# Output projection on half-precision pairs with run-time scales, in a one-core adaLN mixer block

## The chip, the cores and the metric

One NeuronCore of a Trainium2 chip runs the whole program. The metric is the device time of one execution in microseconds. A run of the kernel before has the median 1238.68 us over three executions (1238.41 to 1240.36).

## What is computed

One layer of a transformer block over 2048 latent and 256 context tokens, width 1024, in fp32. Shortened to what matters here:

```python
u = h @ w_in                                  # h: normalised, modulated x
attn = attend(q, k_all, v_all)                # 4 heads, 2048 queries, 2304 keys
br   = concat([silu(gate_a) * attn, silu(gate_p) * pool(pool_in) * pool_scale], -1)   # (2048, 1024)
y    = br @ w_out                             # the output projection: 2048x1024 by 1024x1024
out  = x + gate * y
```

The change touches the last two lines alone. The matmul engine is fed with two-part operands: each fp32 number is written as hi + lo, and a product is made of three passes (hi hi, hi lo, lo hi).

## The kernel before

The program has three stages that overlap at their edges. The feature stage makes `u` feature by feature (`feat`, 48 matrix steps of 48 matmuls each, in four token groups `b`). Its generators of side work (`plan`) are called at numbered steps; step 24 begins the second token group, and the feature stage has 96 steps. Its weights come in through tiles of tag M (6 buffers), are split into fp16 halves with a run-time scale (`split16`, L238 and L239), and from the third group on come back from DRAM (`wd`). Attention (`attn`, `pv_all`) follows. The tail is the output projection.

In the tail the branch outputs lie in DRAM (`brd`), features on partitions. `load_pair(t2)` (L1137) brings the 256 tokens of one pair of token tiles into a tile of tag B (8 buffers), with the residual `xr`. Pair 0 is computed plainly (`plain_pair`, 8 products); pairs 1 to 7 go through `out_pair` (L1196), a Strassen-like form with 7 products, whose operands are sums of blocks of the branch outputs (`sums_of`, 4 VectorE adds) and of blocks of `w_out` (`wo_sums`, the sums T1 to T4). One product (`products`, L1155) is 4 contraction tiles by 3 passes, 12 matmuls of 128x128 by 128x512. An operand is made by `operand` (L1161): ScalarE copies the source to hi in fp32r (L1163), VectorE subtracts for lo (L1164). The weights go through `wo_pair` (L1043) in the same way (L1051 on ScalarE, L1053 on VectorE), two calls per block and 8 blocks. A product is read from PSUM by a VectorE add (`add`, L1199; L1185 in the plain pair; one ScalarE copy, L1210), and `close` (L1144) multiplies by the gate and adds `xr` on GpSimd (L1150), then stores.

`scale_of` (L224) already exists for the feature stage: a matmul with a matrix of ones over columns of sums of squares (L227), a VectorE reduction and a scalar step (L229, L230) and a power on GpSimd (L231). `unscale` is a product and a reciprocal on VectorE (L234, L235); `square` is a ScalarE pass with an accumulator (L248).

The order of instructions in each engine's queue is not the program's: a planner walks the program in its order of priority with cost estimates of its own and puts on each engine the first instruction that it holds ready. The queues are then fixed, and each engine runs its own in order. `order` adds edges by hand (operands of the tail after the last block of attention). All DMAs are issued by SP, in order.

Of the kernel before, what the change touches and what calls it, by code (L numbers as in the profile page):

```python
# [8 lines left out]
F32 = mybir.dt.float32  # L9
F32R = mybir.dt.float32r  # L10
F16 = mybir.dt.float16
AF = mybir.ActivationFunctionType
ALU = mybir.AluOpType
AX = mybir.AxisListType

S, L, D = 2048, 256, 1024
KT = D // 128
# [28 lines left out]
X_AT = {0: "c", 11: 2}  # L46
PROD_AT = {"c": (6, 2), 2: (16, 1), 4: (35, 3), 6: (54, 1)}
GATE_AT = (25, 3)
TW_AT = (3, 2)
KV_AT = 79  # L50
Q_AT = 87
# [8 lines left out]
K_PF = (3, 5)  # L60
WO_AT = (1, 4, 7, 10, 13, 15, 17, 18)
BR_AT = 16
CHUNKS = ((0, 512), (512, 512), (1024, 512), (1536, 512), (2048, 256))
G_A, G_PIN, G_P = 448, 960, 1472

# [2 lines left out]
def tile_hybrid_block(ctx: ExitStack, tc: tile.TileContext, x, c, cx, c_ctx, w_mod, b_mod, norm_g,  # L68
                      w_in, q_lora_g, w_uq, kv_lora_g, w_ukv, q_norm_g, k_norm_g, w_pool,
                      pool_scale, w_out, rope_t, edge_t, out):  # L70
    nc = tc.nc
    x, cx, out = x[0], cx[0], out[0]
    w_mod, w_in, w_uq, w_ukv, w_pool, w_out = (w[0] for w in (w_mod, w_in, w_uq, w_ukv, w_pool, w_out))
# [15 lines left out]
    def st(tag, shape, dt=F32):  # L89
        return sb.tile([128] + list(shape), dt, tag=tag, bufs=BUFS[tag], name=nm(tag))  # L90
# [48 lines left out]
    ssw = cst.tile([128, 20], F32, name="ssw")  # L139
    scl = cst.tile([128, 16], F32, name="scl")  # L140
    unscl = cst.tile([128, 14], F32, name="unscl")
    acs, shs = cst.tile([128, KT, 2], F32, name="acs"), cst.tile([128, KT, 2], F32, name="shs")

    queue = []
# [76 lines left out]

    def scale_of(c, cols, bound=1.0):  # L224

        p = pt("X")
        nc.tensor.matmul(p[:, 0:cols.stop - cols.start], lhsT=ones2, rhs=ssw[:, cols], start=True, stop=True)  # L227
        t = small(1, "sca")
        nc.vector.reduce_sum(t, p[:, 0:cols.stop - cols.start], axis=AX.X)  # L229
        nc.vector.tensor_scalar(out=t, in0=t, scalar1=bound * 2.0 ** -30, scalar2=1e-30, op0=ALU.mult, op1=ALU.add)  # L230
        nc.gpsimd.tensor_tensor(out=scl[:, c:c + 1], in0=t, in1=nhalf[:, 0:1], op=ALU.pow)  # L231
# [6 lines left out]
        nc.scalar.activation(out=hi, in_=src, func=AF.Copy, scale=scale)  # L238
        nc.vector.scalar_tensor_tensor(out=lo, in0=src, scalar=scale, in1=hi, op0=ALU.mult, op1=ALU.subtract)  # L239

    def square(src, c, scale=1.0):
        n = 1
        for k in src.shape[1:]:
            n *= k
        o = junk[:, 0:n]
        if len(src.shape) == 3:
            o = o.rearrange("p (a b) -> p a b", a=src.shape[1])
        nc.scalar.activation(out=o, in_=src, func=AF.Square, scale=scale, accum_out=ssw[:, c:c + 1])  # L248
# [448 lines left out]
    def feat(b):  # L697
# [6 lines left out]
        for g in range(H):  # L704
# [54 lines left out]
                n0 = n1  # L759
            yield  # L760

    def gate_row():
        acc = st("M", [D])
        for k in range(KT):
            yield
            wr = st("M", [D])
            nc.sync.dma_start(out=wr, in_=w_mod[k * 128:(k + 1) * 128, 2 * D:3 * D])
            if k == 0:
                nc.vector.tensor_scalar(out=acc, in0=wr, scalar1=sc[:, 0:1], scalar2=None, op0=ALU.mult)
            else:  # L770
# [42 lines left out]
    g = gate_row()  # L813
    for i in range(10):
        plan.setdefault(GATE_AT[0] + GATE_AT[1] * i, []).append(g)


    K, V, qop = {}, [], {}
# [218 lines left out]
    def load_wo(a, b):  # L1037
# [2 lines left out]
                          .rearrange("(k p) n -> p k n", p=128))  # L1040
        wraw[a, b] = raw

    def wo_pair(key, raw, tag):  # L1043
        if tag == "W":
            w = st("W", [2, 4, 512], F32R)
            wo[key] = (w[:, 0], w[:, 1])
        else:
            wo[key] = (st("B", [4, 512], F32R), st("B", [4, 512], F32R))
        hi, lo = wo[key]
        for k in (0, 2):  # L1050
            a = nc.scalar.activation(out=hi[:, k:k + 2], in_=raw[:, k:k + 2], func=AF.Copy)  # L1051
            order(tail[-1], a.ins, "the last block of attention comes first")
            nc.vector.tensor_tensor(out=lo[:, k:k + 2], in0=raw[:, k:k + 2], in1=hi[:, k:k + 2].bitcast(F32),  # L1053
                                    op=ALU.subtract)
            yield

    def out_weights():
        for a, b in ((0, 0), (0, 1), (1, 0), (1, 1)):
            yield from wo_pair(f"B{a}{b}", wraw[a, b], "W")
# [98 lines left out]
                nc.tensor.matmul(b[:, c0:c1], lhsT=c[:, x0, kt, :], rhs=w[x1][:, kt, c0:c1],  # L1158
                                 start=(first and kt == kts[0] and m == 0), stop=(last_ and kt == kts[-1] and m == 2))

    def operand(src):  # L1161
        c = st("M", [2, 4, 128], F32R)
        nc.scalar.activation(out=c[:, 0], in_=src, func=AF.Copy)  # L1163
        op_last.append(nc.vector.tensor_tensor(out=c[:, 1], in0=src, in1=c[:, 0].bitcast(F32), op=ALU.subtract).ins)  # L1164
        return c

    def blocks_of(br):
        return {f"A{m}{k}": br[:, 4 * k:4 * k + 4, m * 128:(m + 1) * 128] for m in range(2) for k in range(2)}

    def plain_pair(t2, br, xr):  # L1170

        v = blocks_of(br)
        c = {key: operand(v[key]) for key in ("A00", "A10", "A01", "A11")}
        bank = {}
        yield
        for a in range(2):
            for n in range(2):
                for m in range(2):
                    if a == 0:
                        bank[m, n] = pt("A")  # L1180
                    products(bank[m, n], c[f"A{m}{a}"], wo[f"B{a}{n}"], a == 0, a == 1)
                    yield
                    if a:
                        o = st("T", [512])
                        nc.vector.tensor_tensor(out=o, in0=bank[m, n], in1=g[n], op=ALU.mult)  # L1185
                        close(t2, xr, m, n, o, ops=(ALU.add,))

    def sums_of(br):
# [7 lines left out]
    def out_pair(t2, v, xr, early={}):  # L1196
        def add(b, a, c0=0, c1=512):
            o = st("T", [512])
            nc.vector.tensor_tensor(out=o[:, c0:c1], in0=b[:, c0:c1], in1=a[:, c0:c1], op=ALU.add)  # L1199
            return o  # L1200

        for i, a, b in (FORM if t2 > 1 else [FORM[j] for j in (0, 4, 5, 1, 2, 3, 6)]):
            c = early.pop(a, None) or operand(v[a])
            pb = pt("A")
            cols = ((0, 256), (256, 512)) if t2 == 7 and i == 4 else ((0, 512),)
            for c0, c1 in cols:
                products(pb, c, wo[b], True, True, c0, c1)
            if i == 1:
                p1 = st("T", [512])
                nc.scalar.copy(out=p1, in_=pb)  # L1210
            elif i == 6:
                u = add(pb, p1)
            elif i == 5:
                z = add(pb, u)
                if t2 == 1:
                    close(t2, xr, 0, 1, add(p3, z))
            elif i == 7:
                close(t2, xr, 1, 1, add(pb, z))
                y = add(pb, u)
            elif i == 2:  # L1220
                close(t2, xr, 0, 0, add(pb, p1))
            elif i == 3:
                p3 = pb
                if t2 > 1:
                    close(t2, xr, 0, 1, add(pb, z))
            else:
                for c0, c1 in cols:
                    close(t2, xr, 1, 0, add(pb, y, c0, c1), c0, c1)
            yield
# [25 lines left out]
            step += 1  # L1255
    for _ in at:
        pass
    ow = out_weights()
    gb = st("M", [D])
    nc.sync.dma_start(out=gb, in_=gated.partition_broadcast(128))  # L1260
    g = [gb[:, 0:512], gb[:, 512:1024]]
    for n, _ in enumerate(pg):
        for _ in range(WO_AT.count(n)):
            next(ow)
        if n == BR_AT:
            first = plain_pair(0, *pairs.pop())
            next(first)
# [6 lines left out]
    for n, _ in enumerate(first):  # L1274
        if n == 0:
            br, xr = load_pair(1)
        if n < 3:
            next(sums, None)
        elif n == 3:
            early["A00"], early["A01"] = (operand(blocks_of(br)[key]) for key in ("A00", "A01"))  # L1280
            v = sums_of(br)
        elif n == 5:
            early["S4"] = operand(v["S4"])
        else:
            next(sums, None)
    for _ in sums:
        pass
    for t2 in range(1, 8):
        nxt = None
        for n, _ in enumerate(out_pair(t2, v, xr, early)):  # L1290
            if n == 1 and t2 < 7:
                br, nxr = load_pair(t2 + 1)
            if n == 3 and t2 < 7:
                nv = sums_of(br)
        if t2 < 7:
            v, xr = nv, nxr
# [48 lines left out]
```

## Time and profile before

| | us |
|---|---|
| median of three executions | 1238.68 |
| the profiled execution | 1236.57 |
| its span | 1234.8 |
| feature stage and what precedes it | 0 to about 540 |
| attention | about 500 to 1069 |
| output projection on the matmul engine | 1069.3 to 1229.6 |
| TensorE matmul busy | 1169.2 (95%) |
| VectorE / ScalarE / GpSimd busy | 894.6 / 765.8 / 597.3 |

The span is what the profile covers; 1.8 us lie around it. PE is TensorE's matmuls and PEld its weight loads, DVE is VectorE, ACT ScalarE, POOL GpSimd. Durations of matmuls in the profile overlap, so the pace of a stream is read from starts.

### The profile page before, as it was taken

The page shows a single profiled execution, that of the slowest core. Times are in us where ns is not written, and L with a number is a line of the kernel's source. Part 1 is how long each engine was busy: PE and PEld are TensorE (multiplying, and loading weights), DVE is VectorE, ACT ScalarE, POOL GpSimd, SP SyncE. Part 2 cuts the span into 40 slices and gives each one's busy share as a digit, 9 for nine tenths or more (in the row PEclk, how much of TensorE's full clock was granted, in tenths as well). Part 3 has the DMA queues.
Part 4 walks back from the last instruction along what each step waited for, and adds up shares of the span by engine and source line. Part 5 has one row for each costly group of instructions (what it writes and reads, how often), then busy time and mean ns, then how long its engine had stood idle before and what let it go on. Part 6 is the DMA issues. An engine that isn't in the chain of part 4 may idle for free.

```text
span 1234.8 us, 22505 instructions
## 1 busy us (share of the span) xinstructions
PE 1169.2 (95%) x7717; PEld 871.5 (71%) x7717; DVE 894.6 (72%) x1704; ACT 765.8 (62%) x1860; POOL 597.3 (48%) x670
## 2 busy tenths in 40 slices
PE   6899899989999999989999999999999998799998
PEld 2699796877788879655666666666666655688886
DVE  4965766666545445578788888878887866999886
ACT  4587767645655554367777777777777776633221
POOL 3735512624335332024655565565556565236666
PEclk9799899999999999999999999999999999999999
DMA  9446676496435657458977788878888788525532
GB/s 302 143 118 158 165 194 188 131 250 209 144 97 129 150 159 178 125 125 191 230 191 194 168 220 207 191 169 223 203 188 197 197 215 203 181 76 197 188 130 101
DMA packets 192585, 216.82 MB, mean 176 GB/s; under 512 B 92707, under 2 KB 145236, under 8 KB 192342
## 3 DMA queue, kind: packets, MB, share of 16 engines
q1 hardware_dynamic: 192470, 215.38, 65.7%
q8 instruction: 61, 1.00, 0.4%
q14 instruction: 54, 0.44, 0.1%
HBM read 100.33 MB, written 41.85 MB: 115 GB/s over the span
## 4 chain that ended last, share of the span: by engine, by line
PE 71%; DMA 7%; ACT 7%; DVE 6%; SPq 4%; issue 2%; POOL 1%; ACTq 0%; DVEq 0%; POOLq 0%
PE pA L884 19%; PE pA L690 15%; PE pA L1158 13%; PE pO L933 5%; PE pA L340 5%; PE pX L933 5%; SPq L923 3%; PE pX L884 2%; PE pA L619 2%; ACT M L966 2%; ACT T L905 1%; DMA M<-in_w_in_dram 1%; DVE T L371 1%; DMA W<-W 1%; DMA W<-in_w_mod_dram 1%
## 5 line engine op out<-in xcount | busy, mean ns | idle before, releaser
L970 POOL TENSOR_TENSOR M<-W,M 128x512 f16<-128x512 f32 x244 | 277.7, 1160 | 255.3 <-ACT M L966 253.3
L884 PE MATMUL pA<-B,M 128*128 128x512 f16 x1280 | 299.4, 379 | 11.7 <-ACT T L905 9.0
L884 PEld LDWEIGHTS <-M 128*128 128x128 f16 x1600 | 156.1, 98 | 152.2 <-issue 13.5
L908 DVE STREAM_TRANSPOSE W<-T 128x512 f32<-128x512 f32 x310 | 192.9, 641 | 72.4 <-ACT T L905 61.8
L966 ACT ACTIVATE M<-W 128x512 f16<-128x512 f32 x279 | 164.9, 632 | 113.2 <-PE pX L933 45.9
L933 PEld LDWEIGHTS <-B 128*128 128x128 f16 x1728 | 168.4, 98 | 59.7 <-issue 22.5
L690 PE MATMUL pA<-B,B 128*128 128x256 f16 x1728 | 207.0, 274 | 2.4 <-DVE B L239 1.1
L905 ACT ACTIVATE T<-pA,nm,gm 128x512 f32<-128x512 f32 x248 | 188.9, 770 | 16.2 <-DVE nm L893 16.1
L690 PEld LDWEIGHTS <-B 128*128 128x128 f16 x1728 | 167.1, 98 | 31.3 <-issue 5.9
L887 DVE TENSOR_REDUCE mx<-pA 128x1 f32<-128x512 f32 x256 | 169.5, 672 | 16.0 <-PE pA L884 15.6
L933 PE MATMUL pO<-M,B 128*128 128x256 f16 x864 | 114.7, 273 | 9.1 <-ACT M L966 4.4
L1158 PE MATMUL pA<-W,M 128*128 128x512 f32 (+1 forms) x528 | 120.9, 388 | 2.3 <-DVE M L1164 2.3
L933 PE MATMUL pX<-M,B 128*128 128x256 f16 x864 | 112.2, 274 | 5.3 <-DVE M L970 2.7
L1158 PEld LDWEIGHTS pA<-W,M 128*128 128x128 f32 x528 | 98.7, 190 | 22.7 <-DVE M L1164 2.7
L690 PE MATMUL pA<-W,B 128*128 128x256 f32 x576 | 78.1, 288 | 0.0
L690 PEld LDWEIGHTS pA<-W,B 128*128 128x128 f32 x576 | 73.2, 193 | 0.4
L1150 POOL TENSOR_TENSOR B<-T,B 128x512 f32<-128x512 f32 x31 | 50.2, 1623 | 29.5 <-DVE T L1185 27.6
L340 PE MATMUL pA<-W,B 128*128 128x448 f16 (+1 forms) x336 | 64.3, 337 | 0.0
L1150 POOL TENSOR_TENSOR T<-T,M 128x512 f32<-128x512 f32 x27 | 43.0, 1596 | 38.4 <-DVE T L1199 27.7
L1163 ACT ACTIVATE M<-B 128x512 fp32r<-128x512 f32 x32 | 19.7, 628 | 51.3 <-PE pA L1158 38.7
L905 ACT ACTIVATION_READ_ACCUMULATOR T<-pA,nm,gm 128x1 f32 x248 | 48.9, 197 | 0.0
L340 PEld LDWEIGHTS <-B 128*128 128x128 f16 x336 | 31.7, 98 | 22.3 <-issue 0.7
(254 smaller groups left out, 1828.4 us busy)
## 6 DMA issues: line engine op xcount, KB each, us to landing
W<-W SPq DMA_DIRECT2D x496, 144.0 KB
M<-in_w_in_dram SPq DMA_DIRECT2D x24, 512.0 KB
B<-wd SPq DMA_DIRECT2D x24, 512.0 KB
B<-in_x_dram SPq DMA_DIRECT2D x16, 512.0 KB
B<-brd SPq DMA_DIRECT2D x8, 1024.0 KB
B<-in_x_dram SPq DMA_DIRECT2D x8, 1024.0 KB
out_dram<-B SPq DMA_DIRECT2D x31, 256.0 KB
wd<-B SPq DMA_DIRECT2D x12, 512.0 KB
```

Of the source, the lines that this page charges most:

```text
L340: nc.tensor.matmul(p[:, c0:NTOK], lhsT=a[:, kt, k * 128:(k + 1) * 128], rhs=b, start=(kt == 0 and n == 0), stop=(kt == KT - 1 and n == 2))
L690: nc.tensor.matmul(p[:, i * HB:(i + 1) * HB], lhsT=w[:, a, kt, :], rhs=b[:, kt, :], start=(m == 0), stop=(m == 23))
L884: nc.tensor.matmul(b[:, s0:s0 + sn], lhsT=q[:, a, c, p % 2, i], rhs=kt[ki][:, kc, o:o + sn], start=(m == 0), stop=(m == 4))
L887: nc.vector.reduce_max(mx[:, n:n + 1], b[:, :w], axis=AX.X)
L905: nc.scalar.activation(out=e[:, :w], in_=sp[n][:, :w], func=AF.Exp, bias=ng, scale=escale, accum_out=rs[:, n:n + 1])
L908: nc.vector.transpose(TP[p][:, :, i, j0:j1, :].rearrange("p q j b -> p j q b"), e[:, :w].rearrange("p (j q b) -> p j q b", q=4, b=32))
L923: last = nc.sync.dma_start(out=dst[32 * jq:32 * jq + 32, iq], in_=src[32 * iq:32 * iq + 32, jq])
L933: i = nc.tensor.matmul(o, lhsT=V[0][:, j, a], rhs=t[:, c, jj], start=(j == 0 and m == 0), stop=(j == NJ - 1 and m == 2))
L966: a = nc.scalar.activation(out=t[:, 0], in_=s2, func=AF.Copy)
L970: lo = eng.tensor_tensor(out=t[:, 1], in0=s2, in1=t[:, 0], op=ALU.subtract)
L1150: eng.tensor_tensor(out=o[:, c0:c1] if op == ALU.mult else xr[:, k, n, c0:c1], in0=o[:, c0:c1], in1=a[:, c0:c1], op=op)
L1158: nc.tensor.matmul(b[:, c0:c1], lhsT=c[:, x0, kt, :], rhs=w[x1][:, kt, c0:c1], start=(first and kt == kts[0] and m == 0), stop=(last_ and ...
```

## The change

All operands of the output projection become fp16 pairs (hi and lo) instead of fp32r pairs. So that they fit the range of fp16, each is multiplied by a scale: one for the weights, from the sums of squares of all of `w_out`, and one for each pair of token tiles, from the sums of squares of that pair's branch outputs. The product of the two is taken out again where PSUM is read.

- `wo_squares`, new, in the feature stage: 8 loads of 128 rows of `w_out` (512 KB each, tag M) and 8 ScalarE passes for sums of squares, a load and its pass three steps apart, from step 33 to step 78.
- `scale_of(8, ...)` once, for the weights, and `pair_scale(t2, br)` for each pair: two ScalarE passes over 128x1024 elements, one matmul by ones, reduction, scalar step, power on GpSimd, product and reciprocal. It is called for pair 0 in the last steps of attention, for pair 1 after the third product of the plain pair, and for each later pair after the fourth product of the pair before it.
- `wo_pair` and `operand` read the scale on ScalarE and replace the VectorE subtraction by a scalar_tensor_tensor (source times scale, minus hi).
- The PSUM reads become scalar_tensor_tensor with the inverse scale; the ScalarE copy takes it as its scale.
- T1 and T3 take one B buffer each instead of two.

```diff
+WS_AT = (30, 3)
+PS_AT = 11
+    def wo_squares():
+        for k in range(KT):
+            yield
+            raw = st("M", [D])
+            nc.sync.dma_start(out=raw, in_=w_out[k * 128:(k + 1) * 128, :])
+            yield
+            square(raw, k, ssw=sso)
+    g = wo_squares()
+    for i in range(17):
+        plan.setdefault(WS_AT[0] + WS_AT[1] * i, []).append(g)
...
+    def pair_scale(t2, br):
+        for i in range(2):
+            square(br[:, 4 * i:4 * i + 4], 8 + 2 * t2 + i, ssw=sso)
+        scale_of(t2, slice(8 + 2 * t2, 10 + 2 * t2), 4.0, sso, oscl)
+        nc.vector.tensor_tensor(out=ounscl[:, t2:t2 + 1], in0=oscl[:, t2:t2 + 1], in1=oscl[:, 8:9], op=ALU.mult)
+        nc.vector.reciprocal(out=ounscl[:, t2:t2 + 1], in_=ounscl[:, t2:t2 + 1])
...
     def wo_pair(key, raw, tag):
-        if tag == "W":
-            w = st("W", [2, 4, 512], F32R)
-            wo[key] = (w[:, 0], w[:, 1])
-        else:
-            wo[key] = (st("B", [4, 512], F32R), st("B", [4, 512], F32R))
-        hi, lo = wo[key]
+        w = st(tag, [2, 4, 512], F16)
+        hi, lo = wo[key] = (w[:, 0], w[:, 1])
         for k in (0, 2):
-            a = nc.scalar.activation(out=hi[:, k:k + 2], in_=raw[:, k:k + 2], func=AF.Copy)
+            a = nc.scalar.activation(out=hi[:, k:k + 2], in_=raw[:, k:k + 2], func=AF.Copy, scale=oscl[:, 8:9])
...
-            nc.vector.tensor_tensor(out=lo[:, k:k + 2], in0=raw[:, k:k + 2], in1=hi[:, k:k + 2].bitcast(F32),
-                                    op=ALU.subtract)
+            nc.vector.scalar_tensor_tensor(out=lo[:, k:k + 2], in0=raw[:, k:k + 2], scalar=oscl[:, 8:9],
+                                           in1=hi[:, k:k + 2], op0=ALU.mult, op1=ALU.subtract)
...
-    def operand(src):
-        c = st("M", [2, 4, 128], F32R)
-        nc.scalar.activation(out=c[:, 0], in_=src, func=AF.Copy)
+    def operand(t2, src):
+        c = st("M", [2, 4, 128], F16)
+        s = oscl[:, t2:t2 + 1]
+        nc.scalar.activation(out=c[:, 0], in_=src, func=AF.Copy, scale=s)
+        op_last.append(nc.vector.scalar_tensor_tensor(out=c[:, 1], in0=src, scalar=s, in1=c[:, 0], op0=ALU.mult,
+                                                      op1=ALU.subtract).ins)
...
-            nc.vector.tensor_tensor(out=o[:, c0:c1], in0=b[:, c0:c1], in1=a[:, c0:c1], op=ALU.add)
+            nc.vector.scalar_tensor_tensor(out=o[:, c0:c1], in0=b[:, c0:c1], scalar=ounscl[:, t2:t2 + 1],
+                                           in1=a[:, c0:c1], op0=ALU.mult, op1=ALU.add)
...
-                nc.scalar.copy(out=p1, in_=pb)
+                nc.scalar.activation(out=p1, in_=pb, func=AF.Copy, scale=ounscl[:, t2:t2 + 1])
...
+    scale_of(8, slice(0, 8), 4.0, sso, oscl)
...
+        if n == PS_AT:
+            pair_scale(0, pairs[0][0])
...
+        if n == 2:
+            pair_scale(1, br)
...
             if n == 3 and t2 < 7:
+                pair_scale(t2 + 1, br)
                 nv = sums_of(br)
```

## Rows read from the trace of the kernel before

**Rows 1.** Stretches of the tail: busy time (count) of each engine, clock, DMA.

```profile
core 0: us, PE busy (x) PEld busy (x) DVE busy (x) ACT busy (x) POOL busy (x), PEclk, DMA share, GB/s
1069.30:1082.40 13.10, 10.82 (x42) 8.51 (x40) 12.88 (x14) 2.15 (x4) 0.35 (x1) 0.87 0.25 80
1082.40:1106.90 24.50, 24.50 (x109) 20.28 (x108) 24.50 (x26) 11.99 (x15) 7.44 (x4) 1.00 0.14 54
1106.90:1125.94 19.04, 19.04 (x85) 15.77 (x84) 16.86 (x24) 5.22 (x9) 10.46 (x7) 1.00 0.61 199
1144.98:1164.02 19.04, 19.04 (x85) 15.77 (x84) 16.45 (x18) 4.69 (x8) 12.88 (x8) 1.00 0.48 168
```

**Rows 2.** The chain that ended last, from 1060 us on: start, length, what.

```profile
1073.66 8.22 PE pA L1158 x28
1082.59 147.04 PE pA L1158 x660
```

**Rows 3.** Timeline of PE, two neighbouring pairs of the tail: start, length, what.

```profile
1125.95 13.76 PE L1158 MATMUL pA<-W,M 128*128 128x512 f32 x60
...
1144.99 13.76 PE L1158 MATMUL pA<-W,M 128*128 128x512 f32 x60
```

**Rows 4.** The chain in attention: a run of fp16 matmuls with 512 columns.

```profile
635.07 3.24 PE pA L884 x15
```

**Rows 5.** Groups from 1090 us to the end: shapes, count | busy us, mean ns | idle before.

```profile
L1199 DVE TENSOR_TENSOR T<-pA,T 128x512 f32<-128x512 f32 x48 | 32.1, 683 | 15.2 <-PE pA L1158 15.1
...
L1164 DVE TENSOR_TENSOR M<-B,M 128x512 fp32r<-128x512 f32 x26 | 27.2, 1051 | 0.0
```

**Rows 6.** Single lines: duration ns min/median/max, first and last start, shape.

```profile
L1053 DVE TENSOR_TENSOR W<-B,W x12: 1209/1215/2565, 1050.8 to 1098.9; 128x1024 fp32r<-128x1024 f32 x12
...
L239 DVE SCALAR_TENSOR_TENSOR B<-M,scl,B x12: 1271/1284/1761, 187.3 to 281.0; 128x1024 f16<-128x1024 f32 x12
...
L756 DVE SCALAR_TENSOR_TENSOR T<-pO,col,T x20: 476/734/753, 106.0 to 533.8; 128x512 f32<-128x512 f32 x8, 128x260 f32<-128x260 f32 x8, 128x504 f32<-128x504 f32 x4
```

**Rows 7.** The same view: the existing scale and its parts, and the sums of squares.

```profile
L227 PE MATMUL pX<-ssw,ones x6: 165/212/252, 94.2 to 121.5; 128*128 128x2 f32 x4, 128*128 128x4 f32 x2
...
L229 DVE TENSOR_REDUCE sca<-pX x3: 158/158/163, 94.6 to 121.8; 128x1 f32<-128x2 f32 x2, 128x1 f32<-128x4 f32 x1
...
L230 DVE TENSOR_SCALAR sca<-sca x3: 144/153/153, 94.8 to 123.3; 128x1 f32<-128x1 f32 x3
...
L231 POOL TENSOR_TENSOR scl<-sca,nhalf x3: 538/549/550, 96.3 to 124.0; 128x1 f32<-128x1 f32 x3
...
L234 DVE TENSOR_TENSOR unscl<-scl x2: 153/153/153, 124.9 to 125.0; 128x1 f32<-128x1 f32 x2
...
L235 DVE RECIPROCAL unscl<-unscl x2: 137/144/151, 126.7 to 126.8; 128x1 f32<-128x1 f32 x2
...
L248 ACT ACTIVATE junk<-M x12: 1038/1057/1076, 53.2 to 165.7; 128x1024 bf16<-128x1024 f32 x12
L248 ACT ACTIVATION_READ_ACCUMULATOR junk<-M x12: 185/187/217, 54.1 to 166.6; 128x1 f32 x12
```

**Rows 8.** Timeline of all engines around the first operands of pair 2.

```profile
1106.99 0.38 SPq L1139 DMA_DIRECT2D B<-brd  x1
...
1112.40 0.69 DVE L1193 TENSOR_TENSOR T<-B 128x512 f32<-128x512 f32 x1 [1.94 <-DMA B<-brd]
1112.41 0.63 ACT L1163 ACTIVATE M<-B 128x512 fp32r<-128x512 f32 x1 [10.11 <-DMA B<-brd]
```

**Rows 9.** Timeline of PE's matmul row at the start of the tail.

```profile
1073.66 8.22 PE L1158 MATMUL pA<-W,M 128*128 128x512 f32 x28 [2.28 <-DVE M L1164]
```

**Rows 10.** Stretches of the feature stage, columns as in rows 1.

```profile
250.00:300.00 50.00, 46.43 (x368) 37.44 (x367) 31.80 (x50) 24.52 (x56) 15.52 (x29) 0.97 0.87 246
...
400.00:450.00 50.00, 50.00 (x396) 41.04 (x395) 24.83 (x54) 28.88 (x86) 16.59 (x35) 1.00 0.60 154
```

**Rows 11.** PE's longest wait from 240 to 300 us: us in total, times, longest.

```profile
PE pA L690 <- DVE B L239: 0.9, 1, 0.9
```

More of the change, by code (lines that the diff above doesn't have):

```diff
@@ L141, in tile_hybrid_block @@
     unscl = cst.tile([128, 14], F32, name="unscl")
+    sso = cst.tile([128, 24], F32, name="sso")
+    oscl, ounscl = cst.tile([128, 9], F32, name="oscl"), cst.tile([128, 8], F32, name="ounscl")
     acs, shs = cst.tile([128, KT, 2], F32, name="acs"), cst.tile([128, KT, 2], F32, name="shs")
@@ L219, in load_w, with scale_of @@
         wq.append(w)
-    def scale_of(c, cols, bound=1.0):
+    def scale_of(c, cols, bound=1.0, ssw=ssw, scl=scl):
         p = pt("X")
@@ L239, in split16, with square @@
         nc.vector.scalar_tensor_tensor(out=lo, in0=src, scalar=scale, in1=hi, op0=ALU.mult, op1=ALU.subtract)
-    def square(src, c, scale=1.0):
+    def square(src, c, scale=1.0, ssw=ssw):
         n = 1
@@ L1159, in products @@
                                  start=(first and kt == kts[0] and m == 0), stop=(last_ and kt == kts[-1] and m == 2))
-    def operand(src):
-        c = st("M", [2, 4, 128], F32R)
-        nc.scalar.activation(out=c[:, 0], in_=src, func=AF.Copy)
-        op_last.append(nc.vector.tensor_tensor(out=c[:, 1], in0=src, in1=c[:, 0].bitcast(F32), op=ALU.subtract).ins)
+    def operand(t2, src):
[4 more added lines that the diff above has]
+                                                      op1=ALU.subtract).ins)
         return c
@@ L1172, in plain_pair @@
         v = blocks_of(br)
-        c = {key: operand(v[key]) for key in ("A00", "A10", "A01", "A11")}
+        c = {key: operand(t2, v[key]) for key in ("A00", "A10", "A01", "A11")}
         bank = {}
@@ L1184, in plain_pair @@
                         o = st("T", [512])
-                        nc.vector.tensor_tensor(out=o, in0=bank[m, n], in1=g[n], op=ALU.mult)
+                        nc.vector.scalar_tensor_tensor(out=o, in0=bank[m, n], scalar=ounscl[:, t2:t2 + 1], in1=g[n],
+                                                       op0=ALU.mult, op1=ALU.mult)
                         close(t2, xr, m, n, o, ops=(ALU.add,))
@@ L1198, in add @@
             o = st("T", [512])
-            nc.vector.tensor_tensor(out=o[:, c0:c1], in0=b[:, c0:c1], in1=a[:, c0:c1], op=ALU.add)
+            nc.vector.scalar_tensor_tensor(out=o[:, c0:c1], in0=b[:, c0:c1], scalar=ounscl[:, t2:t2 + 1],
+                                           in1=a[:, c0:c1], op0=ALU.mult, op1=ALU.add)
             return o
         for i, a, b in (FORM if t2 > 1 else [FORM[j] for j in (0, 4, 5, 1, 2, 3, 6)]):
-            c = early.pop(a, None) or operand(v[a])
+            c = early.pop(a, None) or operand(t2, v[a])
             pb = pt("A")
@@ L1278, in tile_hybrid_block @@
             next(sums, None)
+        if n == 2:
+            pair_scale(1, br)
+        if n < 3:
+            pass
         elif n == 3:
-            early["A00"], early["A01"] = (operand(blocks_of(br)[key]) for key in ("A00", "A01"))
+            early["A00"], early["A01"] = (operand(1, blocks_of(br)[key]) for key in ("A00", "A01"))
             v = sums_of(br)
         elif n == 5:
-            early["S4"] = operand(v["S4"])
+            early["S4"] = operand(1, v["S4"])
         else:
```

## The prediction

> **What bounds the kernel now.** I read the stretches first, because the change lives in the tail and the shares of the whole span say nothing of it. Up to 1106.9 us VectorE is the bound: it is busy 12.88 of 13.1 us and then 24.5 of 24.5 us, while TensorE's clock is at 0.87 of its upper level in the first of these stretches [rows 1]. From 1106.9 us on TensorE is busy without a gap, 19.04 us for each pair, with VectorE at 16.45, ScalarE at 4.69 and GpSimd at 12.88 us [rows 1]. The chain of waits says the same: its last long piece is 660 matmuls in 147.04 us [rows 2]. So a faster matmul counts from about 1107 us on, and before that more work on VectorE counts.
>
> Two views give the pace. Two neighbouring pairs start 19.04 us apart [rows 3]; a pair is 7 products of 12 matmuls, so one fp32r matmul takes 19.04 / 84 = 226.7 ns. In attention 15 fp16 matmuls of the same shape, each with its own weight load, take 3.24 us, 216.0 ns each [rows 4]. The difference, 10.7 ns, is all that the new type can give a matmul.
>
> **The matmuls.** Pairs 2 to 7 are 6 x 84 = 504 matmuls and run where TensorE is the bound: 504 x 10.7 ns = -5.4 us. The other 192 (plain pair and pair 1) would give 2.0 us more, but VectorE holds them up; I count zero, with -2.0 as the lower bound. Against this come the matmuls by ones. The existing one is two passes of some 0.2 us that overlap in part [rows 7]; I take 0.28 us for both, between 0.2 and 0.4. Five of them (for pairs 3 to 7) fall in the stretch: +1.4 us. Net: **-4.0 us**.
>
> Here the Trainium skill is worth weighing. In attention the fp16 stream goes at 216 ns a matmul [rows 4]. The page "TensorE: Matmul & The Clock Gate", section "Back-to-back issue gap", has for 512 columns both about 216 ns, as the gap of a single matmul, and about 131 ns as a sustained rate of pairs of weight load and matmul. By the second, 504 matmuls would give 504 x (226.7 - 131) ns = 48 us as an estimate, as far as the other engines followed; the stream of this trace agrees with the first.
>
> **VectorE in the steady pairs.** A pair has 7 subtractions for lo and 7 PSUM reads by an add; all become scalar_tensor_tensor. For 1024 elements the new form takes 1284 ns and the old one 1215 [rows 6]. For 512 columns out of PSUM the new one takes 734 (its median, over shapes that are mostly near 512) and the old one 683 [rows 5, 6]. So about +55 ns each, 14 x 0.055 = +0.8 us. The scale adds four small steps, 158 + 153 + 153 + 144 ns = +0.6 us [rows 7]. Sum: 16.45 + 1.4 = 17.9 us, against 84 x 0.216 + 0.28 = 18.4 us on TensorE. It still fits, with 0.5 us to spare instead of 2.6. What eats it is the shared use with GpSimd: the subtraction takes 1051 ns on average in the tail, where the PSUM read of the same shape stays at 683 [rows 5]. The small product reads two operands from SBUF as well, so it may wait for an operation of GpSimd too, at most about 1.1 us, three times the average wait of a subtraction (1051 - 683 = 0.37 us). Bounds: 17.9 to 19.0 us. I take the lower end, since most of such waits show only where VectorE has to run at that moment; the upper end is a rival.
>
> ScalarE gets two passes of 1.06 + 0.19 us for the squares [rows 7], 2.5 us on top of 4.69; GpSimd one power of 0.55 us on top of 12.88. Both stay far below 18.4 us, so they cost nothing as busy time.
>
> **The start of the tail, 1069 to 1126 us.** Here the additions lie on the bound engine. Nine weight splits at +69 ns: 0.6 us. Some 18 subtractions for operands and 18 PSUM reads at +55 ns: 2.0 us. Three scales (pairs 0, 1, 2) at 0.6 us: 1.8 us. Sum +4.4 us. What takes it up: VectorE idles 19.04 - 16.86 = 2.2 us from 1106.9 to 1125.94 [rows 1], of which 1.94 us is a wait for the branch outputs of pair 2, whose load is only issued at 1106.99 us [rows 8]. That load waits for a free B buffer, and the change needs two fewer, so it can be issued earlier. ScalarE's squares for pair 0 come before 1069 us, where the first products wait 2.28 us for VectorE anyway [rows 9]. Net: **+2.0 us**, between 0 (the planner fills the gaps, and the 192 matmuls give their gain back) and +5 (nothing is hidden).
>
> **The feature stage.** Eight loads of 512 KB and eight passes of 1.25 us on ScalarE lie between about 240 and 460 us. From 400 to 450 us TensorE is busy all the time, ScalarE 58% and the DMA engines 60% [rows 10]; there nothing should be late. From 250 to 300 us the DMA engines are at 87% and TensorE has 3.6 us of idle time [rows 10], part of it for a weight split that came just late, 0.9 us [rows 11]; two of the new loads and tiles of tag M fall there, next to the weight loads of the same tag and behind one another in SP's queue. Bounds: 0 and 5 us (the present idle time there and a little more); nothing is removed in this stage, so I see no gain. I take **+1.0 us**, near the lower end, because six of the eight loads lie where there is room. If the cover by the matmuls were gone, the eight passes would cost 8 x 1.25 = 10 us.
>
> **Sum.** -4.0 + 2.0 + 1.0 = -1.0 us on the profiled 1236.57, thus 1235.6. The profiled run lies 2.1 us under the median of 1238.68, so the median comes to **1237.7 us**. A measurement of this kernel can tell about 0.2%, 2.5 us, from no change, and that is how I part faster, same and slower: 1236.2 and 1241.2.
>
> **The rivals.**
> - Faster: the start of the tail hides its additions and the feature stage hides all of its own. Then -4.0 to -6.0, about 1234 us. For it: VectorE's idle 2.2 us, the earlier load of pair 2, room at 400 us. Against: VectorE at 100% for 24.5 us.
> - Slower, the scale on the way to the first operands of a pair. The matmul by ones stands in TensorE's queue; behind it are all products, and it waits for ScalarE's squares, which wait for the load of the pair. In the kernel before ScalarE waited 10.11 us for the load of pair 2 and got it at 1112.41 us [rows 8]. If the load doesn't come earlier, its operands come later by the squares (2.5 us), the matmul (0.28), the small steps with the power (0.3 + 0.55) and hand-overs: about 4 us at a place where VectorE was already late. After such a wait the clock falls: 28 matmuls after the 2.28 us wait took 8.22 us [rows 9] instead of 28 x 0.2267 = 6.35, another 1.9 us. In all about +6 instead of +2 at the start of the tail: 1242 us, up to 1245. It decides if pair 2's branch outputs land after about 1109 us.
> - Slower, the feature stage costs its 5 us: 1241.7.
> - VectorE becomes the bound in all pairs at 18.9 or more: the gain is then 6 x 0.14 = 0.8 us instead of 4.0: 1241.
> - The change doesn't do what it says: fp16 products with another weight tile for each matmul stay at 226.7 ns. Then 5.4 us are missing: 1243.
> - The fp16 matmuls of the tail run so much faster than those of attention that VectorE sets the pace of a pair: 17.9 us instead of 18.4, 6 x 0.5 = 3 us less than the forecast, 1234.7 us. Against it stands the stream of 216 ns [rows 4]. (The Trainium skill's sustained 131 ns, in the section named above, would make this the case; no row here shows such a rate.)
>
> **How the numbers follow.** Forecast (within 0.2%) 0.37, with a range of its own of 1236.2 to 1241.2; faster 0.32; the late scale 0.17; the feature stage 0.06; VectorE as the bound in its worse half 0.05; no gain per matmul 0.02; the far faster matmul 0.01. That makes faster 0.33, same 0.37, slower 0.30. The range goes from 1233 (-6.0 at the start) to 1245 (the late scale at its worst).
>
> **What would show it.** Right: pairs 2 to 7 start 18.4 us apart, with VectorE at 17.9 us busy in each; the first product of pair 2 starts about where it did; TensorE's clock stays at its upper level after 1082 us; 250 to 300 us has no longer idle time than before. Wrong: a wait of TensorE for the matmul by ones or for a lo operand after 1090 us, a stretch at the lower clock there, pairs 19 us apart, or a feature stage that ends over 3 us later.

## The result and the profile after

The kernel after takes 1253.26 us (median of four runs, 1252.19 to 1255.19), against 1238.55 before: ratio 1.0118, interval 1.0106 to 1.0130. The change costs 14.7 us; the forecast was 1237.7, and the range to 1245 missed it. The profiled execution of after took 1252.53 us, its span is 1250.8.

Where the time went is read from the starts of TensorE's matmuls, matched by their place in the program (matrix step of the feature stage, score matmul of attention, product of the tail), after minus before, in us. Matrix steps count from 0 to 47; the steps at which loads are called in the program are the 96 of the plan, two to a matrix step. The profiled run of before lies 2.1 us under its median, and runs of one kernel spread by about 3 us to either side, so a single difference under 3 us is no more than a hint; a jump from one product to the next within a run says more.

| start of | after - before |
|---|---|
| matrix step 12 | -1.3 |
| step 24 / 36 / 47 | +4.4 / +5.4 / +9.6 |
| last score matmul | +8.0 |
| product 0 of the tail | +11.5 |
| product 10 / 11 (pair 1 is products 8 to 14) | +7.8 / +11.1 |
| product 35 (the last of pair 4) | +8.5 |
| product 36 (the first of pair 5) | +16.2 |
| product 57 | +15.2 |

There are two large losses, one in the feature stage and one between products 35 and 36 (7.7 us, and 1.5 more at product 37); a smaller one shows at product 11: in the product before it TensorE waits 2.50 us for the lo half of its operand (L1187). Between the jumps the difference falls by 0.13 us a product, which is 12 matmuls by 10.7 ns: the gain that was forecast.

The stretches of the tail in after (us, busy time and count of each engine, clock, DMA share), to be held against rows 1:

```profile
core 0: us, PE busy (x) PEld busy (x) DVE busy (x) ACT busy (x) POOL busy (x), PEclk, DMA share, GB/s
1080.85:1104.12 23.27, 22.40 (x101) 10.01 (x99) 23.27 (x27) 8.84 (x10) 0.00 (x0) 0.97 0.17 57
1125.79:1144.19 18.40, 18.40 (x89) 8.68 (x88) 16.44 (x25) 7.61 (x14) 15.31 (x10) 1.00 0.46 141
```

Pair 2 takes 18.40 us instead of 19.04, with TensorE busy throughout. At the start VectorE is still busy 100%.

TensorE's waits in after from 1080 us on (total, times, longest), and the timeline around the longest:

```profile
PE pA L1180 <- ACT M L1186: 7.5, 1, 7.5
PE pA L1180 <- DVE M L1187: 3.4, 2, 2.5
PE pA L1180 <- DVE B L1075: 0.6, 1, 0.6
```

```profile
1176.32 0.39 SPq L1162 DMA_DIRECT2D B<-in_x_dram  x1
1176.76 1.45 SPq L1161 DMA_DIRECT2D B<-brd  x1
...
1186.56 1.06 ACT L254 ACTIVATE junk<-B 128x1024 bf16<-128x1024 f32 x1 [16.88 <-DMA B<-brd]
1187.53 0.19 ACT L254 ACTIVATION_READ_ACCUMULATOR junk<-B 128x1 f32 x1
1187.62 0.70 ACT L1186 ACTIVATE M<-B,oscl 128x512 f16<-128x512 f32 x1
...
1188.36 0.75 DVE L1187 SCALAR_TENSOR_TENSOR M<-B,oscl,M 128x512 f16<-128x512 f32 x1 [7.97 <-ACT M L1186]
...
1188.38 4.82 PE L1180 MATMUL pA<-W,M 128*128 128x512 f16 x14 [7.51 <-ACT M L1186]
```

Read from the bottom: the first product of pair 5 waits 7.51 us for the hi half of its operand (L1186). ScalarE has been idle 16.88 us, and what it waits for is not that operand's data but a load of branch outputs, issued at 1176.76 us, for a pass of squares (L254). The pass belongs to pair 7, and in ScalarE's queue it stands ahead of the operands of pair 5. The hi follows at once when the pass is done. After the wait 14 matmuls take 4.82 us, 344 ns each instead of 216; the granted clock is 0.50, its lower level of 1.2 GHz, from 1184.9 to 1191.7 us.

The feature stage, 260 to 280 us, in before, in after and in two of the experiments below (the kernel before with the loads alone, `e6_loads`; the change with the loads later and the passes of the pairs in order, `e8_late`), columns as above:

```profile
260.00:280.00 20.00, 16.43 (x125) 12.46 (x123) 13.31 (x20) 10.90 (x17) 2.94 (x8) 0.91 0.96 266
```

```profile
260.00:280.00 20.00, 15.30 (x77) 8.79 (x76) 13.32 (x20) 9.70 (x16) 5.08 (x12) 0.74 0.90 235
```

```profile
260.00:280.00 20.00, 16.75 (x92) 10.40 (x90) 14.19 (x20) 8.48 (x13) 4.17 (x10) 0.74 0.92 235
```

```profile
260.00:280.00 20.00, 16.79 (x118) 12.20 (x119) 14.44 (x19) 12.63 (x20) 3.72 (x6) 0.91 1.01 268
```

TensorE gets 77 matmuls done instead of 125 (the shapes differ in part), and the granted clock is 0.74 instead of 0.91. These are means over the clock's two levels: the lower one, 1.2 GHz, lasts 10.2 us from 266.7 us on in after, and 3.4 us in before. With the loads elsewhere (last row) both are back. How it comes about, in after's timeline of SP, VectorE and TensorE:

```profile
252.96 0.41 SPq L159 DMA_DIRECT2D M<-in_w_in_dram  x1
253.47 0.62 SPq L782 DMA_DIRECT2D M<-in_w_mod_dram  x1
...
263.46 0.35 SPq L773 DMA_DIRECT2D M<-in_w_out_dram  x1
...
273.63 0.42 SPq L782 DMA_DIRECT2D M<-in_w_mod_dram  x1
```

```profile
260.73 1.28 DVE L786 SCALAR_TENSOR_TENSOR M<-M,sc,M 128x1024 f32<-128x1024 f32 x1 [3.90 <-DMA M<-in_w_mod_dram]
261.94 0.74 DVE L651 SCALAR_TENSOR_TENSOR T<-pX,gqk,T 128x512 f16<-128x512 f32 x1
```

```profile
262.74 0.66 PE L665 MATMUL pX<-ident,M 128*128 128x128 f32 x4 [1.43 <-DVE T L651]
...
265.81 0.41 PE L672 MATMUL pX<-ident,U 128*128 128x128 f32 x2 [2.09 <-DVE U L659]
...
272.48 6.34 PE L346 MATMUL pA<-W,B 128*128 128x448 f16 x21
```

And SP in before:

```profile
247.89 0.67 SPq L153 DMA_DIRECT2D M<-in_w_in_dram  x1
...
253.91 0.38 SPq L767 DMA_DIRECT2D M<-in_w_mod_dram  x1
```

VectorE waits 3.90 us at L786, a step of the gate row that nothing on TensorE needs, for the load that L782 issued at 253.47 us. Behind it in VectorE's queue stand L651, which TensorE does need, and what leads to L659 by way of ScalarE and GpSimd. TensorE waits 1.43 and 2.09 us, its clock falls, and 21 matmuls then take 302 ns each. In before VectorE's longest wait at the same step was 2.0 us.

Why the gate row's load lands so late is not shown. The new load of 263.46 us is no cause of that wait, which had ended by then, and the DMA engines are about as busy as in before (0.91 against 0.87 from 240 to 260 us, 0.90 against 0.96 from 260 to 280). What differs ahead of that load is a weight load of the feature stage: in after it goes out half a us before the gate row's (252.96 us), in before six us before it (247.89). The new load of 238.26 us and its pass of 251.32 lie in front of both. The three other kernels with these loads and passes at these steps (`e1_order`, `e4_sqalone`, `e13_behind`) show the same order and the same wait (3.8 to 3.9 us); with the loads alone the weight load goes out at 248.92 us and the wait is 3.2.

That is not all of the loss. The difference grows by 5.7 us from step 12 to step 24, and by another 4.2 from step 36 to step 47. Of these 3.1 come between steps 44 and 45, at about 500 us, where TensorE waits for the first queries of attention, in after and in before:

```profile
PE pA L903 <- DMA M<-qd: 3.1, 1, 3.1
```

```profile
PE pA L884 <- DMA M<-qd: 2.0, 1, 2.0
```

In after the clock is at 0.50 from 505.6 to 512.4 us; in before it stays at 1.00 there. Why this load comes later was not tried.

### The profile page after: what moved, and what is told of

It reads as the page before. It is cut to its first block, busy times and chain, and to the rows that moved or that the text cites. A ratio compares the mean times of both kernels' runs of the same rounds, so it can differ in the third digit from the quotient of the medians.

```text
span 1250.8 us, 22595 instructions
## 1 busy us (share of the span) xinstructions
PE 1171.1 (94%) x7735; PEld 811.4 (65%) x7735; DVE 900.4 (72%) x1738; ACT 796.0 (64%) x1908; POOL 598.2 (48%) x679
## 4 chain that ended last, share of the span: by engine, by line
PE 59%; DVE 11%; DMA 10%; ACT 9%; issue 4%; POOL 4%; SPq 3%; ACTq 0%; DVEq 0%; POOLq 0%
PE pA L903 20%; PE pA L696 11%; PE pO L952 5%; PE pX L952 5%; PE pA L1180 4%; PE pA L346 4%; PE pX L903 2%; DMA M<-in_w_in_dram 2%; ACT T L924 2%; ACT M L985 2%; SPq L942 2%; DMA M<-in_w_mod_dram 1%; DMA B<-brd 1%; DMA B<-in_x_dram 1%; PE pA L625 1%
## 5 line engine op out<-in xcount | busy, mean ns | idle before, releaser
L903 PE MATMUL pA<-B,M 128*128 128x512 f16 x1280 | 303.0, 382 | 15.1 <-ACT T L924 12.1
L903 PEld LDWEIGHTS <-M 128*128 128x128 f16 x1600 | 156.9, 98 | 158.4 <-issue 20.5
L1180 PEld LDWEIGHTS <-M 128*128 128x128 f16 x696 | 68.3, 99 | 92.5 <-ACT M L1186 8.1
L1180 PE MATMUL pA<-W,M 128*128 128x512 f16 (+1 forms) x528 | 116.4, 380 | 10.9 <-ACT M L1186 7.5
L1186 ACT ACTIVATE M<-B,oscl 128x512 f16<-128x512 f32 x32 | 22.3, 714 | 41.2 <-POOL oscl L237 26.3
```

The costliest lines, as they stand in the source:

```text
L903: nc.tensor.matmul(b[:, s0:s0 + sn], lhsT=q[:, a, c, p % 2, i], rhs=kt[ki][:, kc, o:o + sn], start=(m == 0), stop=(m == 4))
```

## The experiments

Ratios are to the kernel before on the same chip, with the 95% interval. A kernel's profile is set against the profiled run of before in the same way as above.

**One: the passes of pairs 2 to 7 in order.** `e1_order` ties each of them behind the hi half that was made last; the edit bears on ScalarE's order alone, but the planner then orders all queues anew.

```diff
+            if t2 > 1:
+                order(op_hi[-1], q.ins, "squares of a pair come after the operands of the pair before")
```

> The changed kernel, with the sums of squares of pairs 2 to 7 ordered on ScalarE behind the operand that was made last before them in the program. Theory A (a pass of squares for pair 7 stands in ScalarE's queue ahead of the first operand of pair 5 and waits 16.9 us there for its load): the jump of about 9 us at the first two products of pair 5 goes, the time falls from 1253 to about 1244. Rival (the loads of the pairs land too late whatever the order, or VectorE holds the operands up): the wait only moves, 1251 to 1254.

Measured: 1245.67 us, 1.0055 (1.0035 to 1.0074). Products 35 to 36 show no jump, the longest wait of TensorE in the pairs is 2.5 us, the stage before 1069 us is still late (step 47: +7.2, last score matmul: +4.3, against +9.6 and +8.0 in after). The theory held: about 7.8 us were this one place in a queue.

**Two: no sums over the weights.** `e2_nosq` leaves out the eight loads and passes and sets their sums to 1.

```diff
-    g = wo_squares()
-    for i in range(17):
-        plan.setdefault(WS_AT[0] + WS_AT[1] * i, []).append(g)
+    nc.vector.memset(sso[:, 0:8], 1.0)
```

> The changed kernel without the loads and the squares of the weights in the feature stage; the sums of squares of the weights are set to the constant 1 (all else stays). Theory: the feature stage ended 9.6 us later because of them; without them it ends as in the kernel before (within 2 us), 1253 becomes about 1243. Rival (the planner merely put other instructions in another order, and the loss has nothing to do with the loads): the stage stays 5 us or more late, 1248 or above.

Measured: 1247.49 us, 1.0075 (1.0049 to 1.0100), 4 us more than expected. The stage recovered wholly (step 47: -1.6) and the stall at pair 5 stayed (+5.3 at product 36 and 2.3 more at 37), as expected, but the first product came 6.9 us late, which was not expected: the gain was given back in part at the end of attention.

**Three: both.** `e3_both` joins the two edits.

> Both edits together: squares of the pairs ordered behind operands, no loads and squares of the weights in the feature stage (their sums of squares are the constant 1). If the two losses are separate they add up: 1253 - 9 - 10 = about 1234, 4 us under the kernel before, which is what the faster matmul gives. If one of them is only handed on, 1240 or more.

Measured: 1241.48 us, 1.0018 (1.0003 to 1.0034), a miss by 7 us. The last score matmul is 2.9 us late and product 0 is 10.1 late. ScalarE's timeline there:

```profile
1057.89 1.06 ACT L254 ACTIVATE junk<-B 128x1024 bf16<-128x1024 f32 x1 [1.68 <-DMA B<-brd]
...
1059.91 1.06 ACT L254 ACTIVATE junk<-B 128x1024 bf16<-128x1024 f32 x1
...
1065.13 1.06 ACT L254 ACTIVATE junk<-B 128x1024 bf16<-128x1024 f32 x1 [2.07 <-DMA B<-brd]
...
1066.67 0.62 ACT L983 ACTIVATE M<-W 128x512 f16<-128x512 f32 x1
1067.19 1.04 ACT L254 ACTIVATE junk<-B 128x1024 bf16<-128x1024 f32 x1
...
1068.23 1.14 ACT L983 ACTIVATE M<-W 128x512 f16<-128x512 f32 x2
```

Four passes, of pairs 0 and 1, stand among the last halves of attention (L983), two of them with a wait for their load (1.68 and 2.07 us). The code asks for pair 1's passes only in the plain pair.

**Four: the sums over the weights alone**, in the kernel before (`e4_sqalone`).

> The kernel before with nothing but the eight loads and eight passes for the squares of the weights put into its feature stage (their result is not used). If they are the cause of the late feature stage: it ends about 9 us later, 1248. If the loss comes from anything else in the change: 1239 to 1241.

Measured: 1242.57 us, 1.0029 (1.0012 to 1.0045), 5 us under the theory's 1248 and above its rival's 1241. Step 47 starts 7.1 us late, product 0 6.8, product 3 4.7 and the products from 11 on 5.6: the first products of the tail give 2.1 us back, which the expectation had not counted.

**Five: constant scales.** `e5_const` keeps the fp16 operands and the scaled PSUM reads and takes out every load, pass and small step that finds a scale.

```diff
-    scale_of(8, slice(0, 8), 4.0, sso, oscl)
+    nc.vector.memset(oscl[:, 0:8], 2.0 ** -2)
+    nc.vector.memset(oscl[:, 8:9], 2.0 ** 6)
+    nc.vector.memset(ounscl, 2.0 ** -4)
```

> The changed kernel with constant scales: no loads and passes over the output weights, no passes over the branch outputs, no matmuls by ones, no small steps; the fp16 operands and the scaled PSUM reads stay. Theory (all of the loss lies in finding the scales): the feature stage ends within 2 us of the kernel before, the first product of the tail starts within 2 us of it, there is no wait at pair 5, and a pair takes 18.1 to 18.4 us, so the median is about 1233 (1231 to 1236). Rival (the new forms on VectorE at the start of the tail cost the time, whoever makes the scales): the first products still start 5 us or more late, and the time is 1237 to 1241.

Measured: 1234.43 us, 0.9964 (0.9946 to 0.9983). Step 47 0.0, product 0 +2.1, product 11 +2.5, product 57 -3.5. All of the loss lies in finding the scales; what the new forms cost at the start of the tail is at most small (some 2 us by this one profiled run, too little to be read by itself).

**Six and seven: the loads and the passes apart**, in the kernel before. `e6_loads` drops the passes of `e4_sqalone`; `e7_passes` drops the loads and reads resident data.

```diff
-            raw = st("M", [D])
-            nc.sync.dma_start(out=raw, in_=w_out[k * 128:(k + 1) * 128, :])
-            yield
-            square(raw, k, ssw=sso)
+            square(wp_.bitcast(F32)[:, 0], k, ssw=sso)
+            square(wp_.bitcast(F32)[:, 1], 8 + k, ssw=sso)
```

> The kernel before with the eight extra loads of the output weights in the feature stage and no passes over them. Theory (the loads cost, by what they put behind them in the DMA queues): the matrix step 24 starts 2 to 5 us later than before, the last one 5 to 8 us, and the median is 1241 to 1243. Rival (the passes on ScalarE cost): the feature stage stays within 1 us and the median within 1 us of before.

> The kernel before with sixteen passes of 128x512 elements on ScalarE in the feature stage, at the steps of the change's eight passes of 128x1024, over data that lies in SBUF anyway, and without the loads. Theory (the loads cost): the feature stage stays within 1.5 us of before and the median within 1.5 us. Rival (the passes cost): the last matrix step starts 5 us or more later, median 1241 to 1243.

Measured: 1240.04 us, 0.9998 (0.9984 to 1.0012), and 1235.95 us, 0.9968 (0.9951 to 0.9985). The loads alone do lower the clock at 260 us to 0.74 (row above), but the profiled run is only 2.7 us late at step 47, and the median shows no loss: that theory fell as it was put. The passes alone lose nothing; that the kernel with them is 4 us faster no expectation had, and it is not explained (its profiled run is only 1.7 us ahead at the end).

**Eight: pair 1's passes in order too.** `e9_pair1` is `e3_both` with `if t2:` in place of `if t2 > 1:`.

> The changed kernel without the loads and passes over the output weights (their sums set to 1), with the passes over the branch outputs of every pair but the first put behind the newest operand in ScalarE's queue. Against the kernel that did so for pairs 2 to 7 alone, pair 1's two passes leave the end of attention. Theory (passes of pairs 0 and 1 in ScalarE's queue ahead of attention's last halves hold up the end of attention): the first product of the tail starts 4 to 7 us after that of before instead of 10.1, the median is 1237 to 1239. Rival (pair 0's passes alone, or the scale's small steps, hold it up): it stays at 9 us or more and 1241.

Measured: 1238.14 us, 0.9987 (0.9973 to 1.0001); product 0 +5.1 instead of +10.1. The theory held: two passes of 1.25 us and a wait of 2.07, in the wrong place, had cost 3 to 5 us.

**Nine: the whole change with that order** (`e13_behind`: the first edit with `if t2:`).

> The whole change, with the passes over the branch outputs of every pair but the first put behind the newest operand in ScalarE's queue (the run that did so from pair 2 on measured 1.0055 of before). Theory (pair 1's passes held up the end of attention, the loads together with the passes over the weights hold up the feature stage): about 3 us less than that run, ratio 1.002 to 1.005, and the last score matmul still 6 us or more later than before. Rival (once the feature stage is late, the end of attention has room, and pair 1's passes cost nothing): ratio 1.0055 as there.

Measured: 1243.09 us, 1.0029 (1.0012 to 1.0046). The jump at product 11 is gone as well (+11.6, +11.5). The order of the passes is worth 1.0118 - 1.0029 = 0.89%, 11 us, of which about 8 were the stall of pair 5 and about 3 the jump at product 11.

**Ten: the same with the loads later** (`e8_late`).

```diff
-WS_AT = (30, 3)
+WS_AT = (54, 2)
```

> As the kernel with all later pairs' passes behind the newest operand, and the loads of the weights with their passes at steps 57 to 86 in place of 33 to 78. Theory (the loads hurt where the DMA engines are at 0.87 and the gate rows' loads stand behind them, between 250 and 310 us): the matrix steps 24 to 40 start within 1.5 us of before, and the ratio is 0.998 to 1.002. Rival (the loads and passes cost wherever they stand in the feature stage): steps 44 to 47 are 5 us or more late, and the ratio is that of the kernel without the move or worse.

Measured: **1229.76 us, 0.9939 (0.9918 to 0.9960)**, faster than both kernels, and faster than its theory. The clock at 260 us is back at 0.91, step 24 at -3.1, step 47 at -2.7, product 0 at -3.8, product 57 at -7.8. Of this lead 2.7 us stand at step 12 already, before the place of any of the loads. The loads now go out from 348 to 473 us. A late pair in this kernel, where VectorE is nearly full:

```profile
1166.79:1185.05 18.26, 18.26 (x87) 8.45 (x86) 18.16 (x24) 7.80 (x14) 14.20 (x10) 1.00 0.42 150
```

**Eleven: sums of the weights without loads.** `e10_inplace` squares the four tiles of the weights that the tail loads anyway, in the last four rounds of attention.

```diff
+            if p > 27:
+                a, b = WO_PF[p - 2]
+                for i in range(2):
+                    square(wraw[a, b][:, 2 * i:2 * i + 2], 2 * (p - 28) + i, ssw=sso)
```

> As the kernel with all later pairs' passes behind the newest operand, but without the eight extra loads: the passes over the weights read the four tiles of the weights that the tail needs anyway, which lie in SBUF from the last rounds of attention on, in attention's last four rounds. Theory (nothing is left in the feature stage, and ScalarE, busy 77% in attention, has room for 10 us of passes): the same as without any passes over the weights, ratio 0.997 to 1.001. Rival (ten more us on ScalarE at the end of attention are paid there): the last score matmul is 4 us or more later than before, ratio 1.002 to 1.006.

Measured: 1245.00 us, 1.0051 (1.0034 to 1.0069): the rival held. Step 47 is at -0.9, product 0 at +11.1. ScalarE's and TensorE's timelines show the same pattern once more, a pass that waits for its load and a matmul that waits for what stands behind it; the pass is one of pair 0's, and what the passes over the weights cost by themselves is not parted from it:

```profile
1062.81 1.06 ACT L254 ACTIVATE junk<-B 128x1024 bf16<-128x1024 f32 x1 [4.00 <-DMA B<-brd]
```

```profile
1064.49 0.38 PE L949 MATMUL pX<-M,B 128*128 128x256 f16 x2 [3.92 <-ACT M L103]
```

**Twelve and thirteen: two other places for the loads**, with `WS_AT = (50, 2)` and `(58, 2)`, to tell the place from a lucky order.

> As the kernel with the loads at steps 57 to 86 and all later pairs' passes behind the newest operand (ratio 0.9939), with the loads four steps earlier, at steps 53 to 82. Theory (what helps is that the loads are out of the stretch from 250 to 310 us; the exact step doesn't matter): matrix steps 24 to 40 start within 1.5 us of before, ratio 0.992 to 0.998. Rival (that kernel's gain is a lucky order of the planner, not the place of the loads): a ratio of 1.000 or more, with the loss in steps 40 to 47 or at the end of attention.

> The same with the loads at steps 61 to 90. Theory (out of 250 to 310 us is enough): ratio 0.992 to 0.998. Rival (lucky order): 1.000 or more.

Measured: 1233.62 us, 0.9944 (0.9926 to 0.9963), and 1235.17 us, 0.9956 (0.9942 to 0.9971). All three places out of 250 to 310 us give the same within their intervals: it is the place of the loads and their passes, which move together.

**Fourteen: the loads later, the passes of the pairs as in after** (`e16_lateonly`).

> The changed kernel with one edit, the loads at steps 57 to 86: the passes over the branch outputs stay where the planner puts them, ahead of the operands of pairs before. Theory (feature stage and the stall in the tail are two causes that add up): the feature stage ends within 2 us of before, and a product of a pair from 4 on waits 5 us or more for an operand's hi on ScalarE, which stands behind the passes of a later pair that wait for their load; ratio 1.000 to 1.004, some 8 us over the kernel that has both edits. Rival (the stall came from the late feature stage and goes with it): no such wait, ratio 0.994 to 0.996.

Measured: 1241.20 us, 1.0002 (0.9987 to 1.0016). Step 47 is at -2.7, and the stall is there. TensorE's waits from 1080 us on and the line of its timeline:

```profile
PE pA L1180 <- ACT M L1186: 5.1, 1, 5.1
PE pA L1180 <- DVE M L1187: 2.5, 1, 2.5
```

```profile
1174.89 6.87 PE L1180 MATMUL pA<-W,M 128*128 128x512 f16 x24 [5.07 <-ACT M L1186]
```

In `e8_late`, the same but for the order, they are:

```profile
PE pA L1182 <- ACT M L1188: 1.5, 1, 1.5
PE pA L1182 <- DVE M L1189: 0.2, 1, 0.2
```

So the two causes are separate, and within the intervals they add up:

| ratio to before | passes where the planner puts them | passes behind the newest operand |
|---|---|---|
| loads at steps 33 to 78 | 1.0118 | 1.0029 |
| loads at steps 56 to 86 | 1.0002 | 0.9939 |

(The expectations write 57, 53 and 61 for the first of these steps; by the code it is 56, 52 and 60.) The place of the loads, with their passes, is worth 0.9 to 1.2% (11 to 14 us), the order of the passes 0.6 to 0.9% (8 to 11 us). The cells come from different chips, each against before on its own.

## Why the prediction was wrong

**The matmuls, -4.0 us: right.** In `e8_late`, where nothing stalls from pair 2 on, the lead grows from 3.6 us at product 15 to 7.8 at product 57: -4.2 us over the same 504 matmuls and five matmuls by ones. With constant scales (`e5_const`), where there are no matmuls by ones, it is 5.5 us, against 5.4 in the forecast. The pairs of `e8_late` start 18.5 and 18.6, then 18.27 us apart, where the stream of rows 4 had given 18.4. (The "other 192" are 180 in the plain pair and pair 1, and 12 of a product of pair 7 that is cut in two; the term was counted as zero.) The Trainium skill's 131 ns ("TensorE: Matmul & The Clock Gate", section "Back-to-back issue gap") would have made it 84 x 0.131 = 11 us as an estimate, as far as other engines follow; no pair here comes near it.

**VectorE in the pairs, 17.9 us with 19.0 as the upper bound: right as a bound.** In `e8_late` it is busy 18.0 to 18.5 us of a pair (18.16 in the row above), in after 16.44 in pair 2, and TensorE is busy for all but 0.2 us of any of these pairs. Of the two terms of +55 ns one was right and one was not: the PSUM read came to 741 ns in after against 683 (+58), but the product for lo to 984 from a B tile, under the 1051 of the old subtraction:

```profile
L1224 DVE SCALAR_TENSOR_TENSOR T<-pA,ounscl,T 128x512 f32<-128x512 f32 x48 | 35.0, 741 | 5.0 <-PE pA L1180 4.8
L1187 DVE SCALAR_TENSOR_TENSOR M<-B,oscl,M 128x512 f16<-128x512 f32 x28 | 27.4, 984 | 11.0 <-ACT M L1186 11.0
```

**"Both stay far below 18.4 us, so they cost nothing as busy time": the step that failed first.** It priced ScalarE's passes by their busy time, and ScalarE is indeed far from full (7.61 us of 18.40). What costs is the wait that a pass brings with it into a queue that runs in order: 16.88 us of idle ScalarE, of which 7.5 reach TensorE. The Trainium skill states the order in one clause ("PSUM — Partial Sum Buffer", section "Engine vs sequencer instructions": the queues of ScalarE, VectorE and GpSimd are strict FIFO), and the trace agrees: the hi starts at 1187.62 us, when the pass of 1186.56 and its read are done. The rival of the late scale had the mechanism (a pass that waits for its pair's load) but looked for it in the program's order, at pair 2 with pair 2's load. The planner had put pair 7's pass ahead of pair 5's operands. No wait stands at pair 2 in after: its products run through from 1125.79 us. The price of such a wait, 4 us and 1.9 more for the slower clock behind it, was of the right kind: at pair 5 it was 7.5 and 1.5.

**The start of the tail, +2.0 us: wrong for the scales, not contradicted for the new forms.** With constant scales product 0 comes 2.1 us late and product 11 2.5, which one profiled run can't part from the spread. The sentence that pair 0's squares lie where the first products wait for VectorE anyway took only pair 0 for a candidate, and only the time after attention: pairs 0 and 1 both put passes among attention's last halves. With pair 1's moved back product 0 is at +5.1 instead of +10.1.

**The feature stage, +1.0 us, bound 5: a term that was mis-sized.** It measured +9.6 at step 47 in after, and 11 to 14 us by moving the loads with their passes. The two loads in 250 to 300 us were named, and so was the tag that they share (two more go out just outside, at 238.26 and 307.65 us); the price was read from TensorE's own idle time there (3.6 us in rows 10). What was left out is the third party: VectorE's gate step, whose wait for its load holds up what TensorE needs; and the clock, 0.74 over 20 us after two waits of 1.4 and 2.1 us. Left out too was the start of attention at about 500 us, where 3.1 us more are lost. That six of the eight loads lie where there is room was not tried in these words; what the runs show is that from step 56 on all eight together cost nothing that can be measured.

**What stays open.** Loads alone show no loss in the median, passes alone a gain of 4 us, and the two together a loss of 3.6 us. With the passes a tile of tag M is held until its pass is done (the load of 263.46 us until the pass at 290.14), so fewer buffers are left for the loads that matter; that is argued from the times and was not tried alone, nor was the gate step moved by itself. And since each edit makes the planner order all queues anew, about 4 us between two kernels may come from the order alone; the seventh experiment, whose extra passes nothing needs, is the ground for that. The lead of `e8_late`, 7.6 us by the ratio and 9.2 by the medians, is more than that, but its part before the tail (product 0 at -3.8 us) may hold some of it.

## What to carry to other kernels

An instruction added to an engine that is half idle is free only if its data are there when its turn in the queue comes: ask of each one which load it waits for and what stands behind it, and, where a planner chooses the order, look at the queue and not at the program. Small work that is needed late and whose data come late has to be tied behind the work that is needed soon. The added loads with their passes cost 11 to 14 us where the DMA engines were busy 87% of the time and nothing measurable around the stretch with 60% [rows 10]; what such loads cost is read from every engine that waits for a load in that stretch, not from the one that is the bound.

## What was not expected of the hardware

The weight loads of the tail became half as long with fp16, while the pace of the matmuls moved by 10.7 ns only. In before and in after (duration ns min/median/max):

```profile
L1158 PEld LDWEIGHTS pA<-B,M x168: 187/188/188, 1104.4 to 1220.7; 128*128 128x128 f32 x168
```

```profile
L1180 PEld LDWEIGHTS <-M x185: 95/98/181, 1124.9 to 1164.9; 128*128 128x128 f16 x185
```

A weight load of 188 ns is shorter than the 226.7 ns from one matmul to the next, so it could hide behind the matmul already; making it 90 ns shorter moved the pace by no more than 10.7 ns. Short waits are dearer than they look: after 1.43 and 2.09 us of waiting the granted clock was at its lower level for 10.2 us, and for 10.2 us as well with the loads alone, where the longest wait at this place was 1.5 us; in before, with no wait over 0.93 us, it was 3.4 us. After the 7.51 us the next matmuls took 344 ns each.
